# Prompt attention: the transposed probabilities split into two parts straight from PSUM by ScalarE and VectorE

## The chip, the cores and the metric

The kernel runs on one core of a Trainium2 chip. The metric is the device time of one execution in microseconds (us); it was measured three times before the change, with a median of 1506.34 us (1505.44 to 1506.84). The engines are named as in the profile: PE is TensorE, DVE is VectorE, ACT is ScalarE, POOL is GpSimd, SP is the engine that issues most DMAs. PEld is the loading of weights into TensorE, and a small q behind an engine's name stands for its sequencer.

## The reference

The kernel computes one layer of a decoder for a prompt of 1024 tokens and for eight samples of four tokens each. The part that the change touches is the attention of the prompt, 8 heads of 64 dimensions:

```python
def fox_attend(q, k, v, cq, ck, q_pos):
    s = jnp.einsum('bqhd,bkhd->bhqk', q, k).astype(jnp.float32) * (HEAD_DIM ** -0.5)
    bias = jnp.transpose(cq, (0, 2, 1))[..., :, None] - jnp.transpose(ck, (0, 2, 1))[..., None, :]
    ...
    s = jnp.where(mask, s + bias, NEG_INF)
    p = jax.nn.softmax(s, axis=-1).astype(v.dtype)
    return jnp.einsum('bhqk,bkhd->bqhd', p, v)
```

The samples' attention is the same formula over a paged cache of 512 earlier tokens. Around it stand the input projection, a state-space mixer, a gated unit (GLU), the output projection with a LayerNorm, and a feed-forward part.

## The kernel before

All work is in float32. A product that must be exact is done with operands split in two: the value rounded to the float32r type ("hi") and the rest ("lo"), each of which PE takes in one pass. The program is recorded as straight code; a scheduler then orders each engine's instructions by a simulation of readiness, so that the order on an engine is not that of the source. On the chip every engine works through its own list strictly in that order, and waits on semaphores.

The prompt's attention works head by head. `weights(h)` makes the scores of 128 queries at a time in the PSUM tiles `ss` (PE, L863), takes their minimum (DVE, L867 and L869) and writes the exponentials `row` to SBUF (ACT, L873). `values(h)` (L878 to L907) goes over two groups `u` of 512 queries, and for each over the blocks of 128 keys `j`. A block is transposed by PE into a PSUM bank `tw` (L891, one to four matmuls of 128 columns), split into `ph` and `pl`, and multiplied by the values `vv` twice (L900 with `ph`, L901 with `pl`), both adding into the one bank `po`. There are 12 blocks for a head and 96 in all, 48 of them 512 wide and 16 each of 384, 256 and 128. At the end of a group ACT copies the lower half of `po` (`ol`, L904), DVE adds it to the upper half (`oh`), and the result goes to DRAM (`mixd`).

The splitting takes three engines: ACT copies `tw` to an SBUF tile `pe`, DVE casts `pe` to `ph`, and POOL, which works on SBUF alone here, subtracts: `pl = pe - ph`. `tw` has two banks (`psum("psB", s=3, t=2, o=1, f=2)`), `ph` and `pl` three buffers each, `pe` four; `po` is a single bank.

Between the steps of `values` the kernel calls `fill`, which records pieces of two other jobs: first the GLU, then `sample`, the samples' attention in two halves of four samples. `sample` loads pages of the cache by SP (`pg`, L929, six buffers), transposes them (`tk`, L973), makes scores (`ssm`, L981) and multiplies the probabilities by the pages of values (L1026). After the last head comes the output projection (`pso`, L1187): `half(i, k0)` casts an input tile `mx` to `whi` (ACT, L1174) and `wlo`, and the weights `rawo` to `woh` and `wol` (L157 and L82). L82 is the line of the helper `tt`, under which every two-operand operation on DVE and POOL stands; L157 is the cast in the helper `split`:

```python
def split(x, hi, lo, e=V):
    S.copy(hi, x)
    tt(e, lo, x, f(hi), SUB)
```

Of the kernel before, what the change touches and what calls it, by code (L numbers as in the profile page):

```python
# [8 lines left out]
F32 = mybir.dt.float32  # L9
F32R = mybir.dt.float32r  # L10
# [59 lines left out]
def fox_s5_step(tc, a, o):  # L70
    nc = tc.nc
    V, S, G, PE, SY = nc.vector, nc.scalar, nc.gpsimd, nc.tensor, nc.sync
    ctx = ExitStack()

    def pool(name, bufs=1, stack=ctx, side="left", space=None):
        if space is DRAM:
            return stack.enter_context(tc.tile_pool(name=name, bufs=bufs, space=space))
        kw = {} if space is None else {"space": space}
        return stack.enter_context(tc.tile_pool(name=name, bufs=bufs, side=side, reuse_waits="tile", **kw))

    def tt(e, out, x, y, op):
        e.tensor_tensor(out, x, y, op=op)  # L82
# [10 lines left out]
    def f(x):  # L93
        return x.bitcast(F32)

    MUL, ADD, SUB, MAX, MIN = ALU.mult, ALU.add, ALU.subtract, ALU.max, ALU.min
# [16 lines left out]
    def bank(name="x", tag="b"):  # L113
        return cur["pool"].tile([128, 512], F32, tag=tag, name=name, bufs=cur["bufs"][tag])
# [41 lines left out]
# [3 lines that stand above are left out]
# [139 lines left out]
    with ExitStack() as st1:  # L298
# [146 lines left out]
        for dst, order in ((h0, ("state_re", "state_im")), (h0w, ("state_im", "state_re"))):  # L445
            t = ep.tile([128, 2, 2, HD], F32, tag="e", name="h0t")
# [273 lines left out]
        for u in range(3):  # L720
            ps = flip()
            n = 4 if u < 2 else 1
# [155 lines left out]
    def values(h):  # L878
        hs_ = slice(h * 64, h * 64 + 64)
        vr = vs_.pop(h)  # L880
        vv = ap_.tile([128, 8, 2, HD], F32R, tag="vv", name="vv")
        V.tensor_copy(vv[:, :, 0], vr)
        tt(G, vv[:, :, 1], vr, f(vv[:, :, 0]), SUB)
        for u in range(2):
            po = bank("po", "o")
            for j in range(4 * u + 4):
                i0 = max(j, 4 * u)
                n = 512 * (u + 1) - 128 * i0
                t = bank("tw", "t")[:, 0:n]
                for i in range(i0, 4 * u + 4):  # L890
                    PE.transpose(t[:, (i - i0) * 128:(i - i0) * 128 + 128], rows[h, i][:, j * 128:j * 128 + 128], ident)  # L891
                ph = ap_.tile([128, 512], F32R, tag="ph", name="ph", bufs=3)[:, 0:n]
                pl = ap_.tile([128, 512], F32R, tag="pl", name="pl", bufs=3)[:, 0:n]
                pe = ap_.tile([128, 512], F32, tag="pe", name="pe", bufs=4)[:, 0:n]
                S.copy(pe, t)
                V.tensor_copy(ph, pe)  # L896
                tt(G, pl, pe, f(ph), SUB)
                o = po[:, 512 - n:512]
                v = vv[:, j].rearrange("p a d -> p (a d)")
                PE.matmul(o, lhsT=v, rhs=ph, start=(j == 0), stop=False, skip_group_check=True)  # L900
                PE.matmul(o, lhsT=v, rhs=pl, start=False, stop=(j == 4 * u + 3), skip_group_check=True)  # L901
                yield
            ol = ap_.tile([64, 512], F32, tag="ol", name="ol", bufs=1)
            S.copy(ol, po[64:128])  # L904
            oh = ap_.tile([64, 512], F32, tag="oh", name="oh", bufs=2)
            tt(V, oh, po[0:64], ol, ADD)
            SY.dma_start(out=mixd[hs_, u * 512:u * 512 + 512], in_=oh)  # L907
# [209 lines left out]
    ap_ = pool("att", 2, stack=actx)  # L1117
# [9 lines left out]
    for h in range(H - 1):  # L1127
        for j, _ in enumerate(values(h)):
            if j < 4 or j % 2:
                steps(1)  # L1130
            fill(.08 if h < 4 else .3)
            if j == 2:
                vload(h + 1)
            if j == 3 and h + 2 < H:
                loads(h + 2)
    vals = values(H - 1)
    for j in range(4):
        next(vals)
# [73 lines left out]
    t = bank("trl", "t")[0:64, 0:128]  # L1212
# [511 lines left out]
```

## Time and profile before

| | |
|---|---|
| median of three timed runs | 1506.34 us |
| the profiled execution | 1496.75 us |
| its span, first to last instruction | 1494.7 us |
| PE busy in the span | 1386.4 us (93%) |
| DVE, ACT, POOL busy | 1041.9, 583.5, 765.9 us |
| mean granted clock of PE | 0.978 of full speed |

The profiled execution was 9.6 us shorter than the median of the timed ones; around its span lie 2.05 us. The ends of matmuls are modelled in such a profile, so that short waits between them can count as busy. The prompt's attention fills the span from about 335 to 525 us, with the GLU's last products at its start; the output projection follows until about 640 us.

### The profile page before, as it was taken

Reading aid. Unit: us, or ns where it says so; the run is one execution under the profiler, and the core shown is the slowest. Engines: PE = TensorE matmul, PEld = TensorE weight load, DVE = VectorE, ACT = ScalarE, POOL = GpSimd, SP = SyncE. Lnnn points to the kernel's source line nnn. Section 1 sums busy time; section 2 is a strip of 40 time slices with the busy share of each in tenths; the row PEclk is TensorE's granted clock in tenths of the full one; section 3 lists DMA queues with packets and bytes.
Section 4 is the critical chain, followed back from the end, with each engine's and each line's share of the span. In section 5 each row is a group of like instructions: output and inputs, shape, how many; then the busy total and the mean of one; then the engine's idle time right before and its main releaser. Section 6 shows DMA issues by size and latency. Waiting matters only on the chain.

```text
span 1494.7 us, 26764 instructions
## 1 busy us (share of the span) xinstructions
PE 1386.4 (93%) x10023; PEld 1269.9 (85%) x10023; DVE 1041.9 (70%) x1814; ACT 583.5 (39%) x1162; POOL 765.9 (51%) x674
## 2 busy tenths in 40 slices
PE   5897999979999899999999999999979999999986
PEld 3687899877767657799999999999968999999886
DVE  8548589647877844668756455554377888998977
ACT  4332344446766523452333322333245433444212
POOL 3413012025666500048655444444289999999845
PEclk9998999989999999999999999999989999999998
DMA  9354255596784582232234233332363233332212
GB/s 320 136 114 106 77 145 140 164 245 177 188 208 129 157 251 63 77 90 79 91 100 136 95 114 115 100 101 101 117 243 104 72 115 102 101 101 86 71 32 100
DMA packets 199546, 189.20 MB, mean 127 GB/s; under 512 B 43032, under 2 KB 165528, under 8 KB 199416
## 3 DMA queue, kind: packets, MB, share of 16 engines
q1 hardware_dynamic: 193768, 166.66, 38.8%
q0 software_dynamic: 5648, 20.83, 3.5%
q8 instruction: 79, 1.29, 0.4%
q14 instruction: 51, 0.42, 0.1%
HBM read 132.24 MB, written 55.20 MB: 125 GB/s over the span
## 4 chain that ended last, share of the span: by engine, by line
PE 66%; DVE 13%; DMA 6%; POOL 5%; issue 5%; ACT 2%; SPq 2%; DVEq 0%; ACTq 0%; POOLq 0%
PE pd L1399 9%; PE pb L1399 8%; PE mmg L1247 6%; PE pc L1399 6%; PE pa L1399 5%; PE pso L1187 5%; PE mmc L180 5%; DVE pacc L82 2%; DVE x L82 2%; PE ss L863 2%; PE psv L272 2%; POOL s L82 2%; PE mml L1633 2%; PE mme L180 2%; PE tw L891 2%
## 5 line engine op out<-in xcount | busy, mean ns | idle before, releaser
L1399 PE MATMUL pd<-x,a 128*128 128x264 f32 x1344 | 175.2, 288 | 13.2 <-DVE pacc L82 10.3
L1399 PEld LDWEIGHTS pd<-x,a 128*128 128x128 f32 x1344 | 168.6, 190 | 17.2 <-DVE pacc L82 11.6
L157 ACT CAST a<-s 128x256 fp32r<-128x256 f32 (+1 forms) x176 | 84.3, 487 | 221.9 <-PE pd L1399 61.6
L82 DVE TENSOR_TENSOR pacc<-pd,pacc 128x264 f32<-128x264 f32 x360 | 133.0, 422 | 40.5 <-PE pd L1399 40.2
L82 POOL TENSOR_TENSOR pl<-pe,ph 128x512 fp32r<-128x512 f32 (+1 forms) x96 | 102.7, 1078 | 67.8 <-DVE ph L896 49.8
L1399 PE MATMUL pb<-th,a 128*128 128x264 f32 x768 | 134.1, 285 | 0.2 <-DVE v L82 0.2
L1399 PE MATMUL pd<-x,whi 128*128 128x264 f32 x672 | 118.3, 290 | 16.9 <-DVE pacc L82 7.4
L82 DVE TENSOR_TENSOR wlo<-raw,whi 128x1024 fp32r<-128x1024 f32 x68 | 106.2, 1563 | 29.5 <-ACT whi L157 27.4
L1399 PEld LDWEIGHTS pd<-x,whi 128*128 128x128 f32 x672 | 98.8, 192 | 19.8 <-ACT x L157 6.6
L82 POOL TENSOR_TENSOR a<-s,a 128x256 fp32r<-128x256 f32 x112 | 109.6, 990 | 8.7 <-ACT a L157 5.0
L1399 PEld LDWEIGHTS pb<-th,a 128*128 128x128 f32 x768 | 110.4, 188 | 0.7 <-DVE v L82 0.5
L82 DVE TENSOR_TENSOR x<-g,x 128x1056 fp32r<-128x1056 f32 x53 | 99.4, 1882 | 8.0 <-ACT x L157 8.0
L82 POOL TENSOR_TENSOR rs<-rs,mh 128x1 f32<-128x1 f32 (+1 forms) x27 | 19.7, 738 | 158.1 <-DVE rs L86 148.9
L82 POOL TENSOR_TENSOR s<-raw 128x256 f32<-128x256 f32 (+1 forms) x72 | 89.5, 1246 | 19.5 <-DVE a L82 14.9
L180 PE MATMUL mmc<-hhi,whi 128*128 128x352 f32 x288 | 95.3, 331 | 0.0
L180 PE MATMUL mmc<-hhi,wlo 128*128 128x352 f32 x288 | 94.7, 329 | 0.0
L180 PE MATMUL mmc<-hlo,whi 128*128 128x352 f32 x288 | 94.3, 327 | 0.0
L82 POOL TENSOR_TENSOR g<-g 128x1056 f32<-128x1056 f32 x28 | 80.3, 2868 | 11.9 <-PE pb L1399 11.8
L82 DVE TENSOR_TENSOR a<-s,a 128x512 fp32r<-128x512 f32 x64 | 51.0, 805 | 44.5 <-ACT a L157 43.1
L1399 PE MATMUL pb<-tl,a 128*128 128x264 f32 x384 | 80.0, 285 | 0.0
L1399 PE MATMUL pd<-x,wlo 128*128 128x264 f32 x336 | 78.3, 287 | 0.0
L157 ACT CAST whi<-raw 128x1024 fp32r<-128x1024 f32 x48 | 50.5, 1053 | 64.8 <-PE pd L1399 32.4
(466 smaller groups left out, 3966.2 us busy)
## 6 DMA issues: line engine op xcount, KB each, us to landing
g<-gd SPq DMA_DIRECT2D x16, 1056.0 KB
raw<-in_w_up_dram SPq DMA_DIRECT2D x32, 512.0 KB
raw<-in_w_down_dram SPq DMA_DIRECT2D x128, 128.0 KB
pg<-in_cache_k_dram SPq DMA_DIRECT2D x32, 256.0 KB
pg<-in_cache_v_dram SPq DMA_DIRECT2D x32, 256.0 KB
gd<-ca POOLq DMA_DIRECT2D x15, 528.0 KB, 3.0
gd<-cb POOLq DMA_DIRECT2D x15, 528.0 KB, 3.0
raw<-in_w_in_dram SPq DMA_DIRECT2D x12, 512.0 KB
```

What stands on the lines that cost most here:

```text
L82: e.tensor_tensor(out, x, y, op=op)
L157: S.copy(hi, x)
L180: PE.matmul(out, lhsT=wt[:, k], rhs=xt[:, k, c0:c0 + n], start=(k == 0 and i == 0), stop=(k == nk - 1 and i == 2))
L272: PE.matmul(pv[:r], lhsT=x[:, k, t0:t0 + r], rhs=w[:, k], start=(k == 0 and j == 0), stop=(k == KD - 1 and j == 2))
L863: PE.matmul(ps, lhsT=x[0:kk, qs_], rhs=y[0:kk, c * n:(c + 1) * n], start=(kk == 68), stop=(kk == 128))
L891: PE.transpose(t[:, (i - i0) * 128:(i - i0) * 128 + 128], rows[h, i][:, j * 128:j * 128 + 128], ident)
L1187: PE.matmul(ps[:r], lhsT=x[:, k, :r], rhs=w[:, cs_], start=(k == 4 and j == 0), stop=(k == 3 and j == 2))
L1247: PE.matmul(ps, lhsT=wt[:, k], rhs=xt, start=(k == 0 and n == 0), stop=(k == KD - 1 and n == 2))
L1399: PE.matmul(ps[p][:, :PC], lhsT=wt[:, k], rhs=xt[:, k, p * PC:(p + 1) * PC], start=(start and k == 0 and j == 0), stop=(k == n - 1 and j = ...
L1633: PE.matmul(ps, lhsT=wt[:, k], rhs=xt[:, k, c0 - th * HN:c1 - th * HN], start=(fh + k + j == 0), stop=(fh + k == 2 and j == 2))
```

## The change

The tile `pe` and the part of POOL go. `split(t, ph, pl)` takes their place: ACT casts the PSUM bank `tw` to `ph`, and DVE subtracts `ph` from the same bank into `pl`. `ph` and `pl` have four buffers instead of three. Lines behind the change stand three lower: L897 and L898 are the two products, L1023 the samples' product with the values, L1184 and L1171 those of the output projection.

```diff
-                ph = ap_.tile([128, 512], F32R, tag="ph", name="ph", bufs=3)[:, 0:n]
-                pl = ap_.tile([128, 512], F32R, tag="pl", name="pl", bufs=3)[:, 0:n]
-                pe = ap_.tile([128, 512], F32, tag="pe", name="pe", bufs=4)[:, 0:n]
-                S.copy(pe, t)
-                V.tensor_copy(ph, pe)
-                tt(G, pl, pe, f(ph), SUB)
+                ph = ap_.tile([128, 512], F32R, tag="ph", name="ph", bufs=4)[:, 0:n]
+                pl = ap_.tile([128, 512], F32R, tag="pl", name="pl", bufs=4)[:, 0:n]
+                split(t, ph, pl)
```

The scheduler makes a new order of the whole stage from it. Three places follow. The first is PE's list in the second head's first products; `tk` and `ssm` are the samples' work. Before:

```order
L891 MATMUL tw<-cst,row 128x128 x8
L900 MATMUL po<-ph,vv 128x512
L863 MATMUL ss<-kb,qb 128x320
L863 MATMUL ss<-ka,qa 128x320
L863 MATMUL ss<-kb,qb 128x320
L863 MATMUL ss<-ka,qa 128x320
L891 MATMUL tw<-cst,row 128x128 x4
L901 MATMUL po<-pl,vv 128x512
L900 MATMUL po<-ph,vv 128x512
L973 MATMUL tk<-cst,pg 128x128 x4
```

And now:

```order
L897 MATMUL po<-ph,vv 128x512
L863 MATMUL ss<-kb,qb 128x320
L863 MATMUL ss<-ka,qa 128x320
L898 MATMUL po<-pl,vv 128x512
L897 MATMUL po<-ph,vv 128x512
L891 MATMUL tw<-cst,row 128x128 x4
L863 MATMUL ss<-kb,qb 128x320
L863 MATMUL ss<-ka,qa 128x320
L898 MATMUL po<-pl,vv 128x512
L891 MATMUL tw<-cst,row 128x128 x4
L863 MATMUL ss<-kb,qb 128x384
L863 MATMUL ss<-ka,qa 128x384
```

Before, two blocks (`x8`) are transposed ahead of the first product, and the transpositions stand ahead of the product with `pl` of the block two before; now each group of transpositions stands behind that product.

The second place is ACT's list in the last head, where the output projection's casts begin; `rlt` is the transposed sum of the exponentials, `oT` the samples' result. Before:

```order
L895 COPY pe<-tw 128x512 x3
L157 CAST woh_5629<-rawo 128x1024
L895 COPY pe<-tw 128x512
L977 COPY u<-tk 128x512
L895 COPY pe<-tw 128x512
L157 CAST woh_5635<-rawo 128x1024
L895 COPY pe<-tw 128x384
L895 COPY pe<-tw 128x256
L1174 CAST whi<-mx 128x512
L895 COPY pe<-tw 128x128
L1174 CAST whi<-mx 128x512 x3
```

And now:

```order
L157 CAST ph<-tw 128x512
L1036 COPY oT<-tpo 128x4x16
L901 COPY ol<-po 64x512
L157 CAST woh_5453<-rawo 128x1024
L157 CAST ph<-tw 128x512 x2
L157 CAST woh_5459<-rawo 128x1024
L1171 CAST whi<-mx 128x512
L157 CAST ph<-tw 128x512 x2
L1171 CAST whi<-mx 128x512 x3
L157 CAST ph<-tw 128x384
L157 CAST ph<-tw 128x256
L157 CAST ph<-tw 128x128
```

Before, one block (128 wide) stands behind the first cast of `mx`; now five blocks do, two of them ahead of the three other casts of `mx` and three behind.

The third place is PE's list where the samples' last products with the cached values stand. Before, they lie between the products of the output projection:

```order
L1187 MATMUL pso<-wol_5972,whi 128x512
L1187 MATMUL pso<-woh_5971,wlo 128x512
L1026 MATMUL po<-pg,u 32x512 x2
L1187 MATMUL pso<-woh_5617,whi 128x512
L1187 MATMUL pso<-wol_5618,whi 128x512
L1187 MATMUL pso<-woh_5617,whi 128x512
L1187 MATMUL pso<-wol_5618,whi 128x512
L1026 MATMUL po<-pg,u 32x512
```

And now all of them, with the sum `tpo` over the samples' heads, stand inside the prompt's last two heads:

```order
L897 MATMUL po<-ph,vv 128x256
L891 MATMUL tw<-cst,row 128x128
L1023 MATMUL po<-pg,u 32x512
L898 MATMUL po<-pl,vv 128x256
L1023 MATMUL po<-pg,u 32x512
L1023 MATMUL po<-u,pnT 32x512 x4
L1210 MATMUL trl<-cst,rl 64x128
L897 MATMUL po<-ph,vv 128x128
L891 MATMUL tw<-cst,row 128x128 x4
L1033 MATMUL tpo<-cst,om 128x16 x4
L898 MATMUL po<-pl,vv 128x128
L891 MATMUL tw<-cst,row 128x128 x8
```

The samples' work has moved forward in PE's list, and the page loads with it in SP's list; from the middle of the output projection on, the lists of all engines are the same as before, apart from the names of buffers.

## Rows read from the trace of the kernel before

**Rows 1.** The page, its head and part 1: busy time, share, instructions.

```profile
span 1494.7 us, 26764 instructions
PE 1386.4 (93%) x10023; PEld 1269.9 (85%) x10023; DVE 1041.9 (70%) x1814; ACT 583.5 (39%) x1162; POOL 765.9 (51%) x674
```

**Rows 2.** Windows: stretch and length, busy of each engine (instructions), clock, DMA, GB/s.

```profile
335.00:525.00 190.00, 177.78 (x1248) 135.91 (x1247) 150.96 (x323) 122.79 (x327) 112.97 (x111) 0.98 0.66 173
525.00:565.00 40.00, 37.51 (x148) 23.06 (x147) 15.74 (x27) 9.51 (x12) 1.11 (x2) 0.96 0.76 231
640.00:1494.00 854.00, 804.96 (x6476) 794.05 (x6475) 599.62 (x914) 285.59 (x520) 577.27 (x479) 0.99 0.32 103
```

**Rows 3.** Groups by form, 335 to 525 us: busy, mean ns, idle before.

```profile
L82 POOL TENSOR_TENSOR pl<-pe,ph 128x512 fp32r<-128x512 f32 x48 | 64.4, 1350 | 41.9 <-DVE ph L896 35.0 <-PE po L901 5.1 <-PE tw L891 0.9
L896 DVE CAST ph<-pe 128x512 fp32r<-128x512 f32 x48 | 29.5, 627 | 0.6 <-PE po L900 0.2
L895 ACT COPY pe<-tw 128x512 f32<-128x512 f32 x47 | 26.9, 594 | 8.9 <-PE tw L891 7.0 <-POOL pl L82 1.7
L896 DVE CAST ph<-pe 128x384 fp32r<-128x384 f32 x16 | 14.7, 921 | 4.0 <-PE tw L891 1.9 <-ACT pe L895 1.5 <-PE po L900 0.6
L896 DVE CAST ph<-pe 128x256 fp32r<-128x256 f32 x16 | 11.8, 739 | 0.5 <-ACT pe L895 0.5
L896 DVE CAST ph<-pe 128x128 fp32r<-128x128 f32 x16 | 5.1, 320 | 5.1 <-PE po L900 3.9 <-POOL pl L82 0.8 <-ACT pe L895 0.3
```

**Rows 4.** Tile `hlo` at the kernel's start: min, median, max ns; forms.

```profile
L82 DVE TENSOR_TENSOR hlo<-pst,hhi x18: 281/678/692, 15.7 to 81.0; 128x512 fp32r<-128x512 f32 x16, 128x128 fp32r<-128x128 f32 x2
```

**Rows 5.** Line 901, 335 to 525 us: idle time before it, times.

```profile
  issue: 4.4, 13
  POOL pl L82: 2.2, 7
```

**Rows 6.** Line 900, the same view.

```profile
  DVE oh L82: 4.9, 6
```

**Rows 7.** Line 891, the same view.

```profile
  ACT pe L895: 4.5, 9
```

**Rows 8.** Timeline around 416 us: start, length, what, [idle before].

```profile
415.64 0.42 DVE L896 CAST ph<-pe 128x512 fp32r<-128x512 f32 x1
...
416.20 1.27 POOL L82 TENSOR_TENSOR pl<-pe,ph 128x512 fp32r<-128x512 f32 x1 [1.60 <-DVE ph L896]
...
416.45 1.31 DVE L896 CAST ph<-pe 128x512 fp32r<-128x512 f32 x1
```

**Rows 9.** Timeline, one 512-wide block from its transposition to its cast.

```profile
417.85 0.66 PE L891 MATMUL tw<-cst,row 128*128 128x128 f32 x4 [0.76 <-ACT pe L895]
...
419.41 0.60 ACT L895 COPY pe<-tw 128x512 f32<-128x512 f32 x1
...
421.49 0.74 DVE L896 CAST ph<-pe 128x512 fp32r<-128x512 f32 x2
```

**Rows 10.** Windows of line 1026 alone: PE and PEld busy (instructions), clock, DMA.

```profile
525.00:565.00 40.00, 9.06 (x28) 1.27 (x28) 0.96 0.76 231
565.00:640.00 75.00, 2.04 (x12) 0.30 (x12) 1.00 0.26 73
```

**Rows 11.** Timeline of PE in the output projection.

```profile
542.55 1.04 PE L1026 MATMUL po<-pg,u 128*32 128x512 f32 x2 [1.61 <-DMA pg<-in_cache_v_dram]
544.47 1.92 PE L1026 MATMUL po<-pg,u 128*32 128x512 f32 x2 [0.88 <-DMA pg<-in_cache_v_dram]
```

**Rows 12.** Timeline of ACT where the output projection begins.

```profile
514.74 0.62 ACT L1174 CAST whi<-mx 128x512 fp32r<-128x512 f32 x1 [5.65 <-DMA mx<-mixd]
```

**Rows 13.** Timeline of PE at the same place.

```profile
515.41 0.50 PE L1187 MATMUL pso<-woh,whi 128*128 128x512 f32 x1 [2.22 <-ACT whi L1174]
```

## The prediction

> **What bounds the kernel now.** I began with the page's head and busy times: PE is busy for 1386.4 of 1494.7 us [rows 1], so work taken from other engines counts only where PE waits for it. The windows by stage show where that can be [rows 2]. From 640 us on, PE is busy for 804.96 of 854 us, and there the lists are unchanged; nothing of that stretch enters the sum. In the prompt's attention, 335 to 525 us, PE is idle for 190.00 - 177.78 = 12.2 us, DVE is busy for 150.96 us (79%), POOL for 112.97, ACT for 122.79. From 525 to 565 us PE is idle for 2.5 us. Because matmul ends are modelled, these idle times are lower bounds, and I read the waits one by one. Before the products with `pl` the engine stands for 2.2 us on POOL and 4.4 us with no releaser shown [rows 5]; before those with `ph` 4.9 us on `oh`, the single `po` bank [rows 6]; before the transpositions 4.5 us, in 9 waits, on ACT's copy, which frees a bank of `tw` [rows 7]. So the stage is bound by PE's strict order together with the chain from transposition to product, with no engine full. The 96 blocks take 190 / 96 = 1.98 us each, other work included.
>
> **The change part by part.**
>
> *DVE.* The casts go: 29.5 + 14.7 + 11.8 + 5.1 = 61.1 us [rows 3]. In come 96 subtractions with one input in PSUM. The same operation stands at the kernel's start: 678 ns at 512 columns, 281 ns at 128 [rows 4]; in a straight line between these, 546 ns at 384 and 413 ns at 256. That makes 48 x 0.678 + 16 x (0.546 + 0.413 + 0.281) = 32.5 + 19.8 = 52.4 us (46 if the middle widths cost as the smallest, 59 if as the largest). DVE is relieved by 8.7 us. It is not full, and PE waits for it mostly through others; I count a quarter, -2.2 us (0 to -8.7).
>
> The casts cost what they do because of POOL: one of 512 columns takes 0.42 us alone, and 1.31 us when it starts while POOL's 1.27 us subtraction runs [rows 8]; the mean is 627 ns [rows 3].
>
> The Trainium skill, "VectorE: DVE Perf Modes", section "Rules for kernel authors", speaks against the change: an elementwise operation on a matmul's output runs at the single rate from PSUM, and one should copy to SBUF first where several operations follow. By it the undisturbed 0.42 us would be the price of a cast, 48 x (0.678 - 0.42) = 12.4 us would come on DVE at the 512-wide blocks alone, and the term would be +3 instead of -2.2, the sum -2.3 instead of -7.6. The trace's mean of 627 ns does not bear the undisturbed price out, and I keep the row.
>
> *ACT.* The copy of 594 ns [rows 3] becomes a cast of the same bank and shape; I take it as equal, 0 us.
>
> *POOL.* Its subtraction of 1350 ns [rows 3] leaves the path of the second product; what is left of the path is ACT and DVE. The 2.2 us on POOL go, and I take half of the 4.4 us without a releaser as part of the same wait: -4.4 us (-2.2 to -6.6) [rows 5]. What is late next is DVE's own queue, the term after the next.
>
> *The `po` bank.* PE waits 4.9 us for `oh` [rows 6]. The chain that ends a group of queries loses DVE's 128-wide cast of 320 ns and, there as elsewhere, POOL's step after it, and gains one subtraction of 281 ns [rows 3, 4]; `ol` and `oh` themselves stay. I take half: -2.5 us (0 to -4.9).
>
> *The `tw` banks.* This is the new wait. A bank was free when ACT had copied it; now DVE must have subtracted. Behind the waiting transpositions everything on PE is queued, the scores of the next head among it, for which DVE and ACT wait in turn. The new order puts each group of transpositions behind the product with `pl` of the block two before, which needs that very subtraction, so part of the wait falls on a place where PE waits anyway. The 9 waits of today each get one subtraction longer: 9 x 0.678 = +6.1 us [rows 4, 7]. The lower end is 0, when the products' own wait hides it; the upper end is below, under the first rival.
>
> *The samples' work moves forward.* After 525 us PE spends 9.06 + 2.04 = 11.1 us on the samples' products with cached values [rows 10], which now stand inside the attention. They cost nothing where they fall into PE's idle time there, 12.2 us by the windows [rows 2], and full price where not; I take half, -5.5 us (0 to -11.1). In the output projection PE then no longer stops for the pages: 1.61 + 0.88 = -2.5 us [rows 11]. The page loads in SP's list stand earlier with them.
>
> *The end of the attention.* The first cast of `mx` makes ACT idle for 5.65 us, because the transfer is late [rows 12]; PE lost only 2.22 us by it [rows 13], with the samples' work for cover. That cover is gone, and five blocks instead of one now stand behind this cast. If PE loses all of ACT's wait, that is 5.65 - 2.22 = +3.4 us, the value I take (0 to +5.7).
>
> *The sum:* -2.2 - 4.4 - 2.5 + 6.1 - 5.5 - 2.5 + 3.4 = -7.6 us. Against the profiled execution of 1496.75 us that is 1489.1. The timed runs have a median of 1506.34 us, 9.6 us more; the stage is the same in both, so I take the difference off the median: 1498.7 us.
>
> **The rivals.**
>
> *The `tw` banks set the pace (slower).* In one block of the trace the transpositions start at 417.85 us, ACT's copy at 419.41, and its cast is the second of two at 421.49, ending at 422.23 [rows 9], 4.38 us after the start. With the subtraction of 0.68 us in the place of the cast of 0.4 us, its bank would be held for some 4.6 us. Two banks at a pace of 1.98 us a block allow 3.96 us. From that point on each pair of blocks takes the excess, about 0.65 to 0.7 us, or 0.35 us a block; over half of the blocks that is 48 x 0.35 = +17 us. Then the gains at POOL and at `po` are void; the samples' move and the end stay: 17 + 3.4 - 5.5 - 2.5 - 2.2 = +10 us, 1516.5. For it speaks that PE and DVE now wait for each other with only two banks between them, where three and four SBUF buffers stood. Against it: DVE's queue gets lighter, casts of 1.31 us no longer stand ahead, and the path without any queue is far under the limit (0.66 + 0.59 + 0.68 = 1.9 us).
>
> *The path through three engines was the pace (much faster).* `ph` and `pl` had three buffers, and POOL's half of the path is its longest step; POOL itself idled 35.0 us for `ph` of the widest blocks alone [rows 3]. If this loop set the pace, three quarters of PE's 12.2 us go, and all of the samples' work finds room: -9 - 11.1 - 2.5 + 3.4 = -19 us, 1487. Against it: only 2.2 us of PE's waits name POOL [rows 5].
>
> *No room (no change).* PE is 94% busy in the stage by the windows; if the modelled ends hide no slack, the samples' 11.1 us only change their place, and the shorter path is eaten by the banks: -2.5 for the pages, +3.4 at the end, the others against each other, about +1 us, 1507.
>
> **How the numbers follow.** Forecast 0.48, banks 0.25, three engines 0.15, no room 0.12. The forecast's own range, with its terms at half their spread, is 1492 to 1504. A measurement of this kernel can tell 0.2%, 3.0 us, from no change. Faster: 0.43 of the forecast's 0.48, and 0.15, together 0.58. Same: 0.04 of it, 0.02 of the banks' case, and 0.10 of the last, 0.16. Slower: the rest, 0.26. To leave out no more than 2 in 10, the range must reach into both outer cases: 1484 to 1517 us, with the tails of the fastest and of the slowest case outside.
>
> **What would show it.** Right: casts `ph` by ACT near 590 ns, DVE's `pl` near 680 ns at 512 columns and some 52 us in all; POOL nearly empty between 335 and 525 us; no product L1023 and no page wait after the attention; the first `mmg` of the gate some 8 us earlier. The waits before the transpositions should name DVE's `pl`, with some 10 us in all. Wrong: 20 us or more of such waits, an attention that ends later by more than the moved samples' work, or a DVE that is as busy as before. If ACT stands before the first `mx` for longer than 6 us with PE idle beside it, the last term was too small.

## The result and the profile after

The changed kernel is slower: 1523.18 us against 1506.59 us, medians of four runs each, a ratio of 1.0104 with the interval [1.0082, 1.0127]. Measured a second time it had 1520.47 against 1505.83 us, 1.0099 [1.0074, 1.0123]. The forecast was 1498.7 us, with a range to 1517.

The head of the page after and part 1, which answer to [rows 1]:

```profile
span 1520.3 us, 26539 instructions
PE 1404.1 (92%) x10023; PEld 1282.3 (84%) x10023; DVE 1037.0 (68%) x1814; ACT 584.0 (38%) x1162; POOL 658.5 (43%) x578
```

The span is 25.6 us longer, more than the medians differ. To see where, I cut the program at the gate, the first work behind the output projection, whose lists are the same in both. Its row in the kernel before and in the one after (duration, then first and last start):

```profile
L1247 PE MATMUL mmg<-uh,whi x128: 280/285/351, 638.1 to 751.4; 128*128 128x264 f32 x128
```

```profile
L1244 PE MATMUL mmg<-uh,whi x128: 280/285/390, 654.6 to 767.9; 128*128 128x264 f32 x128
```

From the first product of the GLU (304.6 and 303.8 us) to the gate, the stretch that holds the attention and the output projection, it is 333.5 us before and 350.8 after. One profile is not enough here: two more of the kernel before (e13, e14) have 337.4 and 339.4 us, a second of the changed one (e11) 349.6. The means are 336.8 and 350.2 us, 13.4 us apart, with some 3 us of chance to either side. The profile that I forecast from was short in both parts.

Behind the gate the lists are the same, and yet there are 856.6, 858.2 and 866.0 us before and 865.7 and 864.3 after. Most of this difference arises in one place. Some 488 us behind the gate DVE subtracts `wlo = raw - whi` beside a row of POOL's operations without a gap. Before, and after (start, length):

```profile
1126.14 1.30 DVE L82 TENSOR_TENSOR wlo<-raw,whi 128x1024 fp32r<-128x1024 f32 x1 [0.61 <-ACT whi L157]
```

```profile
1142.98 9.32 DVE L82 TENSOR_TENSOR wlo<-raw,whi 128x1024 fp32r<-128x1024 f32 x1 [0.88 <-ACT whi L157]
```

In the second it ends 1.1 us behind the last of POOL's row, and PE stands 5.85 us for DVE's next result. This operation takes 9.3 to 9.9 us in the profiles of all ten runs with the new split (the experiments below included), and of the six with the old one in e8 and e14 alone; in the other four it takes 1.2 to 1.7 us. So up to some 6 us of the difference may lie here. Why it is long in one execution and short in another was not tested, nor is it on record how often the timed runs have it.

The forms of the new path, whole attention (busy, mean ns, idle before), against [rows 3]:

```profile
L82 DVE TENSOR_TENSOR pl<-tw,ph 128x512 fp32r<-128x512 f32 x48 | 32.5, 684 | 21.5 <-ACT ph L157 21.5
L157 ACT CAST ph<-tw 128x512 fp32r<-128x512 f32 x47 | 27.3, 587 | 24.6 <-PE tw L891 24.3
L82 DVE TENSOR_TENSOR pl<-tw,ph 128x384 fp32r<-128x384 f32 x16 | 8.7, 547 | 2.4 <-ACT ph L157 2.4
L82 DVE TENSOR_TENSOR pl<-tw,ph 128x256 fp32r<-128x256 f32 x16 | 6.7, 417 | 4.8 <-ACT ph L157 4.8
L82 DVE TENSOR_TENSOR pl<-tw,ph 128x128 fp32r<-128x128 f32 x16 | 4.5, 284 | 4.6 <-ACT ph L157 4.6
```

Each operation costs what was forecast: 684 ns for 678, and 32.5 + 8.7 + 6.7 + 4.5 = 52.4 us in all. DVE now waits for ACT's `ph`, and ACT for PE's `tw`. The stage's windows, against [rows 2]:

```profile
335.00:525.00 190.00, 179.66 (x1235) 127.43 (x1234) 127.75 (x305) 116.80 (x316) 10.34 (x15) 0.97 0.63 166
525.00:565.00 40.00, 31.05 (x114) 23.11 (x114) 15.22 (x21) 11.27 (x17) 0.00 (x0) 0.87 0.61 180
```

DVE has 23 us less work until 525 us, in part because work has moved behind it (from the GLU's first product to the gate it has 213.2 us, 225.2 before: 12 us less), POOL 103 us less, and PE is as busy as before. The loss shows in the second row: the attention, which ended at 523.6 us, goes on until 549 (with 36 of the output projection's products among its last blocks, 21 before), and PE is busy for 31.05 of 40 us where it was for 37.51. The granted clock there is 0.87. Windows laid on the stretches at the lower clock, before:

```profile
516.97:520.36 3.39, 3.39 (x9) 2.72 (x10) 3.00 (x7) 1.42 (x3) 1.60 (x2) 0.50 0.31 78
544.27:547.67 3.40, 3.20 (x5) 1.34 (x6) 1.23 (x1) 0.60 (x1) 0.00 (x0) 0.50 0.65 173
```

and after:

```profile
423.83:430.64 6.81, 6.28 (x10) 1.66 (x11) 0.00 (x0) 0.00 (x0) 0.00 (x0) 0.50 0.73 239
529.64:533.03 3.39, 3.22 (x11) 2.47 (x11) 0.82 (x3) 1.05 (x1) 0.00 (x0) 0.50 0.89 207
536.47:539.86 3.39, 3.39 (x10) 2.65 (x9) 2.84 (x5) 1.54 (x4) 0.00 (x0) 0.50 0.46 127
550.12:553.51 3.39, 3.17 (x8) 2.50 (x9) 0.17 (x1) 0.00 (x0) 0.00 (x0) 0.50 0.57 144
567.19:573.99 6.80, 5.37 (x13) 4.23 (x14) 3.47 (x5) 2.45 (x4) 0.00 (x0) 0.50 0.33 64
```

Each stretch begins in a wait of PE of 0.8 us or more, or within 1.6 us behind one. Between 400 us and the gate PE has 23.8 us at 1.2 GHz instead of 6.8. But the same view gives 13.7 and 17.1 us in the two more profiles of before and 17.1 in the second of after, so on the mean it is 8 us more; if PE was busy all that time, half of it, some 4 us, is the clock's own price on top of the waits; this is an estimate, and at most that.

Two waits stand out. The first is at the samples' products with pages of values. SP's list, then PE's, at that place:

```profile
411.37 0.45 SPq L840 DMA_DIRECT2D qb<-qd  x1
...
414.42 1.30 SPq L841 DMA_DIRECT2D kb<-kkd  x1
...
417.55 0.39 SPq L848 DMA_DIRECT2D vr<-vd  x1
418.86 5.61 SPq L926 DMA_DIRECT2D pg<-in_cache_v_dram  x6
```

```profile
420.44 0.66 PE L891 MATMUL tw<-cst,row 128*128 128x128 f32 x4 [0.33 <-DVE pl L82]
424.36 2.65 PE L1023 MATMUL po<-pg,u 128*32 128x512 f32 x4 [3.26 <-DMA pg<-in_cache_v_dram]
426.94 0.80 PE L897 MATMUL po<-ph,vv 128*128 128x512 f32 x1
```

The products were moved forward, but the next head's loads stand ahead of their pages on SP, and the first of these loads had itself waited 10.1 us for PE's scores. PE stops for 3.26 us and then works at half clock. The second place is the hand-over to the output projection, ACT's list:

```profile
526.85 1.04 ACT L157 CAST woh<-rawo 128x1024 fp32r<-128x1024 f32 x1 [2.21 <-DMA rawo<-in_w_out_dram]
527.92 1.07 ACT L157 CAST ph<-tw 128x512 fp32r<-128x512 f32 x2
531.85 1.05 ACT L157 CAST woh<-rawo 128x1024 fp32r<-128x1024 f32 x1 [2.85 <-DMA rawo<-in_w_out_dram]
534.97 0.62 ACT L1171 CAST whi<-mx 128x512 fp32r<-128x512 f32 x1 [2.08 <-DMA mx<-mixd]
535.49 1.07 ACT L157 CAST ph<-tw 128x512 fp32r<-128x512 f32 x2
```

Three casts that wait for transfers stand ahead of the last blocks' `ph`; PE stands 2.41 us for `ph` at 528.56 and 2.47 us for `whi` at 535.64 us.

### The profile page after: what moved, and what is told of

It is laid out like the page before. It is cut to its first block, busy times and chain, and to the rows that moved or that the text cites. A ratio compares the mean times of both kernels' runs of the same rounds, so it can differ in the third digit from the quotient of the medians.

```text
span 1520.3 us, 26539 instructions
## 1 busy us (share of the span) xinstructions
PE 1404.1 (92%) x10023; PEld 1282.3 (84%) x10023; DVE 1037.0 (68%) x1814; ACT 584.0 (38%) x1162; POOL 658.5 (43%) x578
## 4 chain that ended last, share of the span: by engine, by line
PE 66%; DVE 13%; issue 6%; DMA 5%; POOL 5%; SPq 2%; ACT 2%; DVEq 0%; ACTq 0%; POOLq 0%
PE pd L1396 9%; PE pb L1396 8%; PE mmg L1244 6%; PE pc L1396 6%; PE pso L1184 5%; PE pa L1396 5%; PE mmc L180 5%; DVE pacc L82 3%; DVE x L82 2%; PE ss L863 2%; PE psv L272 2%; PE mml L1630 2%; POOL s L82 2%; PE mme L180 2%; PE tw L891 2%
## 5 line engine op out<-in xcount | busy, mean ns | idle before, releaser
L1396 PEld LDWEIGHTS pd<-x,a 128*128 128x128 f32 x1344 | 172.2, 194 | 20.1 <-DVE pacc L82 17.0
L82 DVE TENSOR_TENSOR wlo<-raw,whi 128x1024 fp32r<-128x1024 f32 x68 | 118.3, 1740 | 30.3 <-ACT whi L157 27.7
L82 POOL TENSOR_TENSOR a<-s,a 128x256 fp32r<-128x256 f32 x112 | 106.3, 961 | 19.9 <-ACT a L157 12.2
L82 DVE TENSOR_TENSOR x<-g,x 128x1056 fp32r<-128x1056 f32 x53 | 95.3, 1804 | 9.3 <-ACT x L157 9.3
L82 POOL TENSOR_TENSOR vv<-vr,vv 128x512 fp32r<-128x512 f32 x8 | 12.0, 1501 | 153.6 <-DVE vv L882 111.0
L82 DVE TENSOR_TENSOR pl<-tw,ph 128x512 fp32r<-128x512 f32 (+1 forms) x96 | 52.1, 550 | 33.3 <-ACT ph L157 33.3
```

Of the source, the lines that this page charges most:

```text
L1396: PE.matmul(ps[p][:, :PC], lhsT=wt[:, k], rhs=xt[:, k, p * PC:(p + 1) * PC], start=(start and k == 0 and j == 0), stop=(k == n - 1 and j = ...
```

## The experiments

Two theories. *Order*: the split costs nothing; the new order of the lists does. *Split*: the bank held until DVE has subtracted does. In most kernels the order of an engine's list was fixed by edges that demand an order of issue and no wait (shortened):

```python
for row in ORDER:                 # one row for each engine fixed: places in the recorded program
    for x, y in zip(row, row[1:]):
        tc.add_manual_dep(ins[y], ins[x].name, NoSync)
```

What each gave, the ratio to the kernel before measured beside it, with its interval, and the stretch from the GLU's first product to the gate in its profile:

| kernel | ratio of times | stretch, us |
|---|---|---|
| before | 1 | 333.5, 337.4, 339.4 |
| changed | 1.0104 [1.0082, 1.0127], 1.0099 [1.0074, 1.0123] | 350.8, 349.6 |
| e1_order | 1.0078 [1.0048, 1.0107] | 345.1 |
| e2_swap | 1.0197 [1.017, 1.0225] | 365.0 |
| e3_casts_last | 1.0035 [1.0018, 1.0052] | 343.0 |
| e4_three_banks | 1.0348 [1.0306, 1.039] | 383.7 |
| e5_pages | 1.0062 [1.0037, 1.0086] | 350.0 |
| e6_handover | 1.0036 [1.0017, 1.0055] | 341.5 |
| e7_both | 1.0007 [0.999, 1.0024] | 335.2 |
| e8_before_handover | 0.9963 [0.9945, 0.998] | 335.7 |
| e9_before_best | 0.998 [0.9962, 0.9999] | 334.4 |
| e10_split_best | 1.003 [1.0012, 1.0047] | 335.3 |
| e12_products_last | 1.0084 [1.006, 1.0107] | 347.4 |

**e1_order**: the new split; rows for PE and SP from the kernel before.

> The changed kernel, with the lists of PE and SP from the attention to the output projection put back into the order that they had before the change; ACT and DVE are ordered anew. Order theory (the split itself costs nothing, the loss of 16.6 us comes from the samples' products and the page loads that moved forward and from the new hand-over to the output projection): 1500 to 1509 us, PE waits for pages below 1 us in the attention. Split theory (a bank held until DVE has subtracted costs the time): 1516 to 1525 us, with waits of PE's transpositions for DVE's pl well above the 0.5 us that the changed kernel shows.

Measured: 1518.72 us. The order theory in its plain form falls. PE's waits in front of the transpositions, 335 to 525 us:

```profile
  DVE pl L82: 21.6, 24
```

That is 17.1 us more than the 4.5 us of [rows 7]. In the old order the waits for the banks are PE's largest, as the first rival had it. The stretch is 8.3 us longer than the mean of before, so about half of them stand where PE lost time before too.

**e2_swap**: the old split; rows for PE, ACT, DVE and SP from the changed kernel.

> The kernel before, with its splitting by three engines kept, but PE, ACT, DVE and SP in the order that the change brought (copy of tw at the place of the new cast, DVE's cast at the place of the new subtraction). Order theory: 1515 to 1525 us, with the page wait and the half clock near 420 us and the half clock between 525 and 575 us as after the change. Split theory: 1503 to 1510 us.

Measured: 1535.02 us, some 14 us more than the new split in the same order. PE's waits name POOL, 335 to 525 us:

```profile
PE po L901 <- POOL pl L82: 7.6, 16, 0.9
```

So the split theory falls too. Each splitting suits its own order, and costs 11 to 14 us in that of the other. What is left is to ask what the new order does wrong.

**e3_casts_last**: the changed kernel in its own order, with this in ACT's list and the like on DVE and PE:

```diff
 L157 CAST woh_5459<-rawo 128x1024
-L1171 CAST whi<-mx 128x512
 L157 CAST ph<-tw 128x512 x2
-L1171 CAST whi<-mx 128x512 x3
 L157 CAST ph<-tw 128x384
 L157 CAST ph<-tw 128x256
 L157 CAST ph<-tw 128x128
+L1171 CAST whi<-mx 128x512 x4
```

> The changed kernel in its own order, but the first four casts whi, their subtractions, the two products mx x rb and the 36 products pso that stand among the last blocks of the attention are moved behind the attention's last block on ACT, DVE and PE. If the hand-over is a main part of the loss (ACT standing for mx in front of the last blocks' casts): the attention ends 6 to 10 us earlier than 549 us and the time is 1514 to 1519 us. If it is not: 1521 to 1526 us.

Measured: 1510.63 us, less than expected: 0.64 to 0.69% less than the changed kernel, about 10 us; the profile gives 7. The last product `pl` starts at 541.2 us, and PE goes over to the output projection without a gap:

```profile
541.16 0.33 PE L898 MATMUL po<-pl,vv 128*128 128x128 f32 x1
541.35 0.50 PE L1184 MATMUL pso<-woh,whi 128*128 128x512 f32 x1
```

Of the four stretches at half clock behind 525 us one is left, of 3.4 us.

**e12_products_last** takes that edit apart: only PE's 36 products go behind the last block, ACT and DVE keep their lists. PE's list begins so:

```diff
 L891 MATMUL tw<-cst,row 128x128 x4
+L897 MATMUL po<-ph,vv 128x512
+L898 MATMUL po<-pl,vv 128x512
...
+L898 MATMUL po<-pl,vv 128x128
 L1184 MATMUL pso<-woh_5441,whi 128x512
```

> The changed kernel in its own order, but only the 36 products pso that stand among the attention's last blocks on PE are moved behind the last block; ACT, DVE and SP keep their lists, so the casts of mx still stand in front of the last blocks' casts. If the products are what matters (kept back, they cover the wait for the later output weights): 1509 to 1513 us, as with the casts moved too. If ACT's casts in front of the last blocks are what matters: PE loses its filler beside them, 1519 to 1526 us. In between, 1514 to 1518 us, both count.

Measured: 1517.13 us. So some 3 of the 10 us come with the products alone, and most of them, some 7, with the casts of `mx` on ACT and the steps behind them on DVE (taken apart in this one order only). PE in the profile:

```profile
530.50 0.61 PE L897 MATMUL po<-ph,vv 128*128 128x512 f32 x1 [2.28 <-ACT ph L157]
...
538.35 0.80 PE L897 MATMUL po<-ph,vv 128*128 128x512 f32 x1 [3.24 <-ACT ph L157]
```

**e5_pages**: the changed kernel, three products later in PE's list:

```diff
 L891 MATMUL tw<-cst,row 128x128 x4
-L1023 MATMUL po<-pg,u 32x512 x2
 L897 MATMUL po<-ph,vv 128x512
 L898 MATMUL po<-pl,vv 128x512
 L897 MATMUL po<-ph,vv 128x512
-L1023 MATMUL po<-pg,u 32x512
 L898 MATMUL po<-pl,vv 128x512
+L1023 MATMUL po<-pg,u 32x512 x3
```

> The changed kernel in its own order, but three of the samples' products with pages of values (the two at which PE stood 3.26 us near 421 us, and the one behind them) stand two blocks of the attention later on PE; nothing else is moved. If the late pages and the half clock behind them are the second part of the loss: the wait goes and with it the stretch at half clock from 423.8 to 430.6 us, 3 to 6 us less than the changed kernel, 1517 to 1520 us. If the wait only changes its place: 1521 to 1525 us.

Measured: 1514.14 us, some 6 us less than the changed kernel. Half of the wait is left:

```profile
426.47 2.29 PE L1023 MATMUL po<-pg,u 128*32 128x512 f32 x6 [1.62 <-DMA pg<-in_cache_v_dram]
```

and the window around it is at full clock (0.91 in the changed kernel):

```profile
400.00:440.00 40.00, 36.97 (x238) 21.77 (x236) 23.93 (x59) 21.12 (x59) 1.28 (x1) 1.00 0.75 198
```

In this one profile the stretch up to the gate is hardly shorter, 350.0 us, since it has 10.2 us at half clock from 528 us on. With the hand-over mended, the same edit shortens it by 6.3 us (341.5 to 335.2, e6 to e7), and the time by 4.3 us.

**e7_both**: the edits of e5 and e6 (below) together.

> Both edits together, the three products with pages two blocks later and the hand-over with all its casts behind the attention's. If the two parts are independent and the split itself costs next to nothing: 1500 to 1506 us, level with the kernel before or faster. If the split itself costs some microseconds in every order: 1508 to 1514 us.

Measured: 1506.99 us, level with the kernel before, also by the profile (335.2 us against a mean of 336.8). Mending the two places takes the loss away. It does not bring the forecast gain, and it does not show that the whole loss came from them: the control e8 below gains by the first mend too.

**e6_handover** and **e10_split_best** move the casts `woh` as well: the third and fourth each behind two more blocks, then, on top of e7, the fourth behind all blocks. ACT's list against e3, and then against e7:

```diff
+L157 CAST ph<-tw 128x512 x2
 L157 CAST woh_5453<-rawo 128x1024
 L157 CAST ph<-tw 128x512 x2
 L157 CAST woh_5459<-rawo 128x1024
-L157 CAST ph<-tw 128x512 x2
```

```diff
+L157 CAST ph<-tw 128x384
+L157 CAST ph<-tw 128x256
+L157 CAST ph<-tw 128x128
 L157 CAST woh_5459<-rawo 128x1024
-L157 CAST ph<-tw 128x384
-L157 CAST ph<-tw 128x256
-L157 CAST ph<-tw 128x128
```

> As the kernel with the casts of mx behind the attention, and the third and fourth cast woh of the output weights, for which ACT stood 2.0 and 3.2 us in front of the attention's casts, each behind two more blocks' casts on ACT (wol likewise on DVE). If ACT's list is what delays the last blocks: the attention ends 3 to 5 us earlier than there, the loads of the other four rows of weights start earlier by as much, and the time is 1505 to 1509 us (1510.6 there). If the transfers set the end: within 2 us of 1510.6.

> The changed kernel with both edits, and besides the fourth cast woh of the output weights, for which ACT stood in front of the casts of the last three blocks (PE stood 2.75 and 0.66 us for them), behind these casts on ACT and DVE. If that wait and the stretch at half clock behind it (6.83 us) are what is left of the loss: 4 to 6 us less than the 1507.0 us without it, 1501 to 1503 us. If the late weights set the end of the hand-over anyway: 1505 to 1509 us.

Measured: 1511.27 us, no better than e3; and 1509.32 us, no better than e7. Neither brought the gain that was looked for; the branch in which late transfers set the end holds for e6 and, within 0.4 us, for e10. In e10 the waits of PE for `ph` shrink to 0.35 us and less, and come back behind them:

```profile
529.88 0.51 PE L1184 MATMUL pso<-woh,whi 128*128 128x512 f32 x1 [1.97 <-ACT whi L1171]
544.44 1.20 PE L1184 MATMUL pso<-woh,whi 128*128 128x512 f32 x4 [1.54 <-ACT woh L157]
```

**e4_three_banks**: `psum("psB", s=2, t=3, o=1, f=2)` in the changed kernel, in the order that the scheduler makes of it.

> The changed kernel with three banks for tw and two for the scores (instead of two and three). The scheduler then pulls the samples further forward still (first product with a page of values after 28 blocks instead of 35). Split theory (two tw banks are too few): 1500 to 1510 us. Order theory: the pages are late as before or more, 1515 to 1530 us; the ends of the samples come well ahead of the output projection, which may take some of the hand-over's loss away.

Measured: 1561.15 us. A bank taken from the scores, and samples pulled forward still more, cost far more than expected. PE's waits, 335 to 600 us, spread over many causes, of which I show the first two, so this run doesn't tell the bank from the order:

```profile
PE pso L1184 <- ACT woh L157: 6.7, 2, 4.4
PE po L1023 <- DMA pg<-in_cache_v_dram: 4.7, 2, 2.7
```

**e8_before_handover** is the control: the kernel before, with the edit of e3 on its own lists (21 products on PE). ACT's list:

```diff
-L1174 CAST whi<-mx 128x512
 L895 COPY pe<-tw 128x128
-L1174 CAST whi<-mx 128x512 x3
+L1174 CAST whi<-mx 128x512 x4
```

**e9_before_best** adds a shift of eight samples' products with pages to places 28 to 36 products `pso` later; on PE, each pair so:

```diff
-L1026 MATMUL po<-pg,u 32x512 x2
 L1187 MATMUL pso<-woh_5971,whi 128x512 x4
...
 L1187 MATMUL pso<-wol_5630,whi 128x512
+L1026 MATMUL po<-pg,u 32x512 x2
```

> The kernel before in its own order, but its one cast of mx that stood among the attention's last blocks, its subtraction, one product mx x rb and the 21 products pso are moved behind the attention's last block, as in the edit of the changed kernel. There only one 128-wide block stood behind that cast. If the number of blocks behind the cast is what makes the hand-over dear: within 3 us of the kernel before, 1503 to 1510 us. If it is the products of the output projection that are kept as cover for the later weights: 5 us or more faster, 1497 to 1502 us.

> The kernel before with the hand-over edit, and besides eight of the samples' products with pages of values, at which PE stood 3.52 and 0.82 us in the output projection, 28 to 36 products pso later. If a page wait costs its own length and half of the stretch at half clock behind it (6.83 us there): 4 to 8 us less than the 1500.8 us of the kernel without this edit, 1493 to 1497 us. If the wait only moves, or the loads queued behind the pages on SP come late instead: 1499 to 1504 us.

Measured: 1500.83 us and 1502.84 us. e8 is faster than both kernels of this study; e9 adds nothing. By the expectation's second branch, then, the number of blocks behind the cast is not what makes the hand-over dear: the same mend gives 5.6 us where one small block stood there. Of e3's 10 us only the difference, some 4 us, belongs to the change (6 by the stretches: 7.2 us in e3, 1.1 in e8).

With the same mends the new split stays behind the old one: e7 is 6.2 us slower than e8, e10 6.5 us slower than e9, with stretches up to the gate that differ by 0.5 and 0.9 us. Where these 6 us lie no run shows. The operation `wlo` behind the gate is a candidate: it is long in e10 and short in e9; but in the profiles of e7 and e8 it is long in both.

In e8 the attention's last product starts at 514.2 us, 9 us earlier than before, and PE then stands for pages:

```profile
542.37 1.05 PE L1026 MATMUL po<-pg,u 128*32 128x512 f32 x2 [3.52 <-DMA pg<-in_cache_v_dram]
544.23 1.92 PE L1026 MATMUL po<-pg,u 128*32 128x512 f32 x2 [0.82 <-DMA pg<-in_cache_v_dram]
```

In e9 that wait has turned into one for the weights:

```profile
545.54 2.07 PE L1187 MATMUL pso<-woh,whi 128*128 128x512 f32 x4 [5.69 <-ACT woh L157]
```

**e11_after_again** is the changed kernel without an edit, **e13_before_again** and **e14_before_third** the kernel before without one, for a profile alone.

> The changed kernel as it is, once more, beside the others. If the 16.6 us hold: 1519 to 1526 us. If part of it was the luck of the four runs: 1512 to 1518 us, and the two edits taken together would then explain all of it and more.

> The kernel before as it is, for a second profile. If the first one is typical up to the gate: the gate starts 333 to 335 us behind the first product of the GLU (638.1 - 304.6 = 333.5 us there), and the 5.6 us of the kernel before with the mended hand-over don't lie in that stretch. If the first one was short by luck: 336 to 340 us, and the mended one (335.7 us) gains there.

> The same for a third profile: 333 to 335 us if the stretch repeats, up to 340 us if it varies.

Measured: e11 1520.47 us, so the loss holds; e13 and e14 337.4 and 339.4 us up to the gate, so the first profile was short by luck. The products are the same; what differs is the clock; the window of its longest stretch at the lower level in e14:

```profile
512.49:522.73 10.24, 9.61 (x51) 6.60 (x51) 6.74 (x14) 2.64 (x5) 3.13 (x4) 0.50 0.78 211
```

Near that place the first profile had 3.4 us of it. Against these two, e8 (335.7 us) gains 2 to 4 us up to the gate; the rest of its 5.6 us is not located. In e6 to e10 and e12 four products of the feed-forward part also stand earlier on PE; that makes 0.5 us in their profiles, behind the gate.

## Why the prediction was wrong, step by step

*DVE, ACT.* The sizes were right: 52.4 us of subtractions, 587 ns for 594. The Trainium skill, "VectorE: DVE Perf Modes", section "Rules for kernel authors", has elementwise work read PSUM at the single rate; the trace fits it, with 684 ns against the 0.42 us of an undisturbed cast from SBUF [rows 8], though these are two operations, so that the pair doesn't single out PSUM. The price did not decide: with 12 us less work DVE gave PE nothing that the runs show.

*POOL, the `po` bank* (-4.4 and -2.5). The waits named there went, and others took their place. PE's idle time in front of the products with `pl`, 335 to 525 us, against [rows 5]:

```profile
  issue: 3.1, 5
  DVE pl L82: 2.9, 8
```

and in front of those with `ph`, against [rows 6]:

```profile
  issue: 5.8, 12
  ACT row L873: 3.1, 6
  POOL vv L82: 1.0, 2
  DVE oh L82: 0.9, 2
```

`oh` fell from 4.9 to 0.9 us; waits for `row` and without a releaser came instead. Counting a wait that goes as time that goes was the error in both terms, 6.9 us together.

*The `tw` banks* (+6.1). In the changed kernel the wait is smaller than before, against [rows 7]:

```profile
  DVE pl L82: 1.2, 3
```

The new order puts the transpositions behind the product with `pl`, which needs the same subtraction. The wait that I and the first rival reckoned with stands in the old order (e1: 21.6 us, 17.1 more than before). The rival had the mechanism, but for a program that doesn't run, and the 17 us that it priced as time came there as waits, while the stretch grew by 8.3 us.

*The samples' work moves forward* (-5.5 and -2.5) **failed.** I took the products as filler that is ready, and let the pages go along "in SP's list". They stand there behind a head's loads. The term has the wrong sign, and this is the largest error: -8.0 us forecast, and e5 gives some 6 us back (4 from e6 to e7) by placing three products two blocks later; the same kind of edit on the kernel before (e9) gives nothing. Even e7, with that wait halved, is only level with before.

*The end of the attention* (+3.4, at most +5.7) was right in sign, and near in size by luck. I priced the old wait of the first cast of `mx` alone, 5.65 us; after the change it is 2.08 us, and the casts `woh` in front of it wait for transfers instead, 2.21 and 2.85 us, where it was 0.78 and 0.63 before. PE stood with ACT, and the clock went down. Mending the place gives 7 (profile) to 10 us (timed; e3), most of it by the casts (e12), but on the kernel before as well 1 to 6 us (e8); the change's own part is 4 to 6 us.

*The rest.* The measured loss is 15 to 17 us. The pages (4 to 6) and the hand-over (4 to 6) make 8 to 12 of it; the rest stays open, with `wlo` behind the gate as a candidate. No term looked there, since the lists are the same.

*The signs and the rivals.* Of the signs of being wrong one came: the attention ends 25 us later, far more than the 11.1 us of moved work; the bank waits stayed at 1.2 us. "No room" comes nearest once both places are mended: e7 is level with before. Against "Three engines were the pace" speaks the same e7, which is no faster. The slower case had a chance of 0.25 and came nearest in time, 1516.5 us, but for a reason that the changed program avoids.

## What to carry to other kernels

When a change lets a scheduler reorder, price the places where instructions that wait for a transfer now stand ahead of the critical chain on an in-order engine; here 12 us less work on DVE did not pay for them. Look on the loading queue at what is issued ahead of the data that moved work needs. And test an edit and its order apart: put the old order under the new code and the new order under the old. Try every mend on the old kernel too: here over half of one mend's gain in time, 5.6 of 10 us, had nothing to do with the change.

## What the runs showed of the hardware

I had not expected the clock to make runs of one kernel so unlike: the same lists had 6.8, 13.7 and 17.1 us at 1.2 GHz between 400 us and the gate. A wait of 3.26 us was followed by 6.8 us at 1.2 GHz, one of 1.62 us at the same place by none (e5), and the waits of 2.28 and 3.24 us of e12, with single products and shorter waits between them, lie around a stretch of 20.5 us at half clock that begins at 530.7 us. Nor had I looked for one DVE subtraction of two SBUF tiles, 128x1024, to take 1.30 us in one execution of the kernel before and 9.41 us in another (e14), POOL being busy beside it both times.
